# Two blocks of a head as one group, spatial products in pairs, and the last half row undivided

## The chip, the cores and the metric

The kernel runs on one core of a Trainium2 chip. The metric is device time in microseconds (us), the median of several runs; lower is better. The kernel before takes 609.88 us (three runs, 609.84 to 611.01). Engines: PE multiplies matrices (PEld is its loading of weights), DVE and ACT work on vectors, POOL is the general engine, SP issues most of the DMAs. Each engine takes its instructions strictly in the order in which they stand in its queue, so an instruction that waits holds up all behind it.

## The reference

One layer on 512 tokens of width 1024. `h = x @ w_in` is split into nine parts; branch A is a gated MLP that mixes tokens within chunks of 128, branch B is attention with two softmax maps per head.

```python
ua = gelu(ua); va = layer_norm(gelu(va), a_ln_g, a_ln_b)
sa = einsum("gts,bnsgc->bntgc", tril(w_s), va_chunks) + b_s      # 8 groups, 4 chunks
ya = ua * sa * silu(za)
q = rope(qh) * DK ** -0.5; k = rope(kh)                          # 8 heads, 2 maps, 64 wide
# for each block of 128 queries, causal:
pr = softmax(where(mask, q @ k.T, -inf)); a = pr[0] - lam * pr[1]; o = a @ v
yb = rms_norm(o, b_subln_g) * 0.8 * silu(zb)
merged = sigmoid(ga) * (ya @ w_branch_a) + sigmoid(gb) * (yb @ w_branch_b)
x = layer_norm(alpha * x + merged @ w_out + sigmoid(x @ w_ple_gate) * (p @ w_ple), ln_g, ln_b)
```

## The kernel before

All large products are made in three parts, each operand split into a high and a low piece (`three`, L279); each part is one matmul of 128 x 128 weights and 512 columns, counted by `product` (L267). These products are the stream of work on PE. Everything else is hung into the stream by hand: `later(n, fn)` (L262) puts a function on an agenda that `product` calls once n more products have been issued. What the function issues then stands at that place in every engine's queue. The numbers in the tables at the top are thus counts of products. No scheduler moves anything afterwards.

In the order of the stream: k and q of the first two heads with their rotary turn (`rope`, L694), two feature groups of ua, then v and zb (`quad`, L627: a product of halves in seven steps), then for the other three pairs of heads k, q and ua (`feature_group`, 24 products each, 144 products a pair), then za (8 x 24 products). Attention is spread over this last stretch, from the end of zb to the end of za. Then come va, ga, gb, pg, the embedding, wb, wa and the output product.

Attention works by head h and block i of 128 queries. `scores` (L763) multiplies q with k for (i + 1) x 128 keys, two maps with two matmuls each, into two `sc` banks of PSUM; DVE adds the mask and takes the row's extreme (L776, named CUSTOM_DVE_ANT_0 in the trace), ACT makes the exponentials and their sums (L782). `combine` (L786) merges the two maps on DVE (L794). `transposes` (L798) turns the result by 128 x 128 pieces into the `tr` bank and ACT copies it out as `at`. `values` (L808) multiplies it with v into the `po` bank, whose four quarters belong to the four blocks. After a head's last block, `squares` (L818), `norm`, `scale` (on POOL) and `gated` (DVE) make the normalised and gated output, and `turned` (L853) transposes it. `attention` (L871) makes a list of starts, one for each of the 32 blocks, from PERIOD (13, 16, 20, 23 products between them, 72 in all; shortened by STRETCH, 0.78, in the last two heads), and `block` (L860) hangs the steps of one block: scores at its start e, `combine` COMBINE[i] products behind, transposes at start e + 2, values at start e + 3. So at one start PE does the values of one block, the transposes of the next and the scores of the one after that; such a place, where PE leaves the stream of products and comes back, is called a point below. TAIL and LAST_TAIL (heads 5 to 7) say how far behind the last values the four steps of a head stand; `turned` stands at the start nine further.

`spatial` (L1130) makes the token mixing of branch A, one call for each of 8 groups, 17 products apart, during the product of ga: four f32 matmuls into `po` or `tr`, and 4 products later two DVE instructions that read the bank.

The output product works by rows t of 128 tokens. `fill` (L1331) has ACT put what is to be added into a bank, the first halves (512 columns) of all rows are made in two groups, then the second halves row by row. The second half of the last row is two pieces of 256 columns, each with its own bank and 24 products. Behind each piece stands `stats` (bn_stats on DVE, L1351), behind each row `last_norm` (L1353): aggregate, power on POOL, centring and scaling with the gains, and a store by SP. The last row is stored in two pieces of 512 columns.

Of the kernel before, what the change touches and what calls it, by code (L numbers as in the profile page):

```python
# [49 lines left out]
PERIOD = (13, 16, 20, 23)  # L50
COMBINE = (10, 11, 13, 12)
LAST_TURNS = (14, 27, 45)
PAIR = 144
TAIL = (2, 14, 26, 44, 56)
LAST_TAIL = (2, 10, 20, 32, 42)
# [6 lines left out]
SPATIAL = (194, 17)  # L62
# [26 lines left out]
FILL = ((14, 0, 1), (20, 2, 0), (24, 1, 1), (44, 3, 0), (110, 2, 1), (124, 3, 1), (150, 3, 2))  # L89
# [144 lines left out]
def hybrid_layer(ctx: ExitStack, tc: tile.TileContext, a, out: bass.AP):  # L234
# [528 lines left out]
    def scores(h, i):  # L763
        n = (i + 1) * P
        q, k0, k1 = stacks["q", h], stacks["k", h], stacks["kx", h]
        sc = [pbank("sc", 2) for _ in range(2)]
        for m in range(2):
            for o, kk in enumerate((k0, k1)):
                pe.matmul(sc[m][:, :n], q[:, m, i * P:(i + 1) * P], kk[:, m, :n],  # L769
                          start=o == 0, stop=o == 1)  # L770
        pr = [ap_.tile([P, T], F32, name=f"p{m}", tag=f"p{m}", bufs=3) for m in range(2)]
        if i == 0:
            todo["st", h] = small([P, NT, 4], "sth", 2)
        st = todo["st", h][:, i, :]
        for m in range(2):
            dve.tensor_tensor_reduce(out=pr[m][:, :n], in0=sc[m][:, :n], in1=mask[:, T - n:],  # L776
                                     scale=-(DK ** -0.5), scalar=3e38, op0=OP.add, op1=OP.min,
                                     accum_out=st[:, m:m + 1])
            if m == 0:
                dve.tensor_scalar(out=st[:, 0:1], in0=st[:, 0:1], scalar1=-math.log(T),  # L780
                                  scalar2=None, op0=OP.add)
            act.activation(pr[m][:, :n], pr[m][:, :n], AF.Exp, bias=st[:, m:m + 1], scale=-1.0,  # L782
                           accum_out=st[:, 2 + m:3 + m])
        todo[h, i] = pr, st

    def combine(h, i):  # L786
        n = (i + 1) * P
        pr, st = todo[h, i]
        r1 = small([P, 1], "r1")
        dve.reciprocal(out=r1, in_=st[:, 3:4])  # L790
        rho = small([P, 1], "rho")
        dve.tensor_scalar(out=rho, in0=r1, scalar1=st[:, 2:3], scalar2=neglam[:, 0:1],
                          op0=OP.mult, op1=OP.mult)
        dve.scalar_tensor_tensor(out=pr[0][:, :n], in0=pr[1][:, :n], scalar=rho[:, 0:1],  # L794
                                 in1=pr[0][:, :n], op0=OP.mult, op1=OP.add)
        todo[h, i] = pr[0]

    def transposes(h, i):  # L798
        n = (i + 1) * P
        ad = todo[h, i]  # L800
        tr = pbank("tr", 1)
        for j in range(i + 1):
            pe.transpose(tr[:, j * P:(j + 1) * P], ad[:, j * P:(j + 1) * P], ident)  # L803
        at = ap_.tile([P, T], F32, name="at", tag="at", bufs=2)
        act.activation(at[:, :n], tr[:, :n], AF.Copy)  # L805
        todo[h, i] = at

    def values(h, i):  # L808
        at = todo.pop((h, i))
        if i == 0:  # L810
            todo["po", h] = pbank("po", 1)
        po = todo["po", h]
        for j in range(i + 1):
            pe.matmul(po[:, i * P:(i + 1) * P], at[:, j * P:(j + 1) * P],  # L814
                      v[:, j, h * P:(h + 1) * P], start=j == 0, stop=j == i)

# [43 lines left out]
    def block(h, i, starts):  # L860
        e = NT * h + i
        later(starts[e], scores, h, i)
        later(starts[e] + COMBINE[i], combine, h, i)
        later(starts[e + 2], transposes, h, i)
        later(starts[e + 3], values, h, i)
        if i == NT - 1:
            tail = TAIL if h < 5 else LAST_TAIL
            for d, fn in zip(tail, (squares, norm, scale, gated)):
                later(starts[e + 3] + d, fn, h)

    def attention():  # L871
        starts = []
        for h in range(NH):
            stretch = 1.0 if h < NH - 2 else STRETCH
            at = PAIR * (h // 2) + BEGIN + h % 2 * sum(PERIOD) * stretch
            for n in PERIOD:
                starts.append(round(at))
                at += n * stretch
        starts += [starts[-1] + n for n in LAST_TURNS]
        for h in range(NH):  # L880
            for i in range(NT):
                block(h, i, starts)
# [247 lines left out]
    def spatial(g):  # L1130
# [13 lines left out]
        later(4, gated)  # L1144
# [5 lines left out]
    for g in range(KT):  # L1150
        later(SPATIAL[0] + SPATIAL[1] * g, spatial, g)
# [176 lines left out]
    last_columns = [[(0, T), (T, D)] for _ in range(NT - 1)] + [[(0, T), (T, T + T // 2), (T + T // 2, D)]]  # L1328
# [39 lines left out]
    zst = [small([P, 2 if t < NT - 1 else 3, 6], "vst", 4) for t in range(NT)]  # L1368
# [25 lines left out]
    for t in range(NT):  # L1394
# [11 lines left out]
        later(1, last_norm, t, [slice(0, D)] if t < NT - 1 else [slice(0, T), slice(T, D)])  # L1406
# [42 lines left out]
```

## Time and profile before

| what | value |
|---|---|
| median of the runs | 609.88 us |
| the profiled execution | 610.13 us |
| its span, first to last instruction | 608.2 us |
| TensorE clock granted, mean | 0.997 |
| busy share: PE, DVE, ACT, POOL | 99%, 76%, 57%, 21% |
| instructions of PE | 2880 |

Each row of a timeline gives the start and the length of an instruction in us, its engine, its line, what it writes and reads, and in brackets the idle time of the engine before it, with what ended that. A matmul's end is modelled, and the next starts before it; what a stream of matmuls costs is read from start to start. An f32 matmul (attention's values and the spatial products) stands as two instructions in the trace. A wait shows as idle time in front of the instruction that waited.

### The profile page before, as it was taken

What the parts mean: (1) busy time and instruction counts of PE and PEld (TensorE: products, weight loads), DVE (VectorE), ACT (ScalarE), POOL (GpSimd) and SP (SyncE); (2) the same over time, 40 slices, a digit from 0 to 9 for tenths busy, and PEclk for the clock granted to TensorE, in tenths of its full rate; (3) what the DMA queues carried; (4) which work ended last, traced back from release to release, by engine and by line L of the source; (5) the groups of instructions that cost most, each with busy time, mean ns of one, the idle gap of its engine ahead of it and who ended that gap; (6) DMA issues with size and microseconds to landing.
All of it is one profiled execution on the core that took longest, in us unless ns stands there. A gap on an engine that the chain in (4) does not pass through costs nothing.

```text
span 608.2 us, 8270 instructions
## 1 busy us (share of the span) xinstructions
PE 600.1 (99%) x2880; PEld 503.1 (83%) x2880; DVE 464.8 (76%) x770; ACT 346.7 (57%) x537; POOL 125.4 (21%) x133
## 2 busy tenths in 40 slices
PE   9999999999999999999999999999999999999995
PEld 6888888888888888888888888888888888888885
DVE  6995645588789789678965788779687887879476
ACT  6656475755745745746676666554776565555310
POOL 1234121041252432422110321331120011110011
PEclk9999999999999999999999999999999999999998
DMA  8689899697887896892579988976999578997002
GB/s 309 228 246 182 252 205 227 237 240 252 277 208 277 273 258 230 240 313 61 150 310 288 305 241 217 273 175 191 286 244 306 172 206 250 253 256 288 27 35 103
DMA packets 44541, 138.23 MB, mean 227 GB/s; under 512 B 5940, under 2 KB 7092, under 8 KB 44148
## 3 DMA queue, kind: packets, MB, share of 16 engines
q1 hardware_dynamic: 34436, 102.97, 46.8%
q0 software_dynamic: 9488, 34.35, 30.6%
q8 instruction: 22, 0.36, 0.2%
q10 hardware_dynamic: 576, 0.39, 0.2%
q14 instruction: 19, 0.16, 0.1%
HBM read 118.69 MB, written 29.49 MB: 244 GB/s over the span
## 4 chain that ended last, share of the span: by engine, by line
PE 98%; DVE 1%; DMA 0%; DVEq 0%; issue 0%
PE ps_pp L268 56%; PE ps_sc L268 22%; PE ps_tx L268 9%; PE ps_sc L769 3%; PE ps_po L814 3%; PE ps_tr L803 1%; PE ps_po L268 1%; PE ps_tr L268 1%; PE ps_tr L1133 1%; PE ps_po L1133 1%; PE ps_tx L857 1%; DMA xr<-in_xT 0%; PE ps_po L1319 0%; PE ps_tr L1319 0%; DVE base L1361 0%; DVE xl L295 0%
## 5 line engine op out<-in xcount | busy, mean ns | idle before, releaser
L392 DVE TENSOR_TENSOR wl<-wr,wh 128x1024 fp32r<-128x1024 f32 x133 | 165.4, 1250 | 36.7 <-ACT wh L389 36.5
L389 ACT ACTIVATE wh<-wr 128x1024 fp32r<-128x1024 f32 x133 | 139.4, 1054 | 68.7 <-PE ps_pp L268 20.5
L268 PE MATMUL ps_pp<-xh,wh 128*128 128x512 f32 x232 | 91.2, 394 | 0.0
L268 PE MATMUL ps_pp<-xh,wl 128*128 128x512 f32 x232 | 91.0, 393 | 0.0
L268 PE MATMUL ps_pp<-xl,wh 128*128 128x512 f32 x232 | 90.4, 391 | 0.1
L365 POOL DMA_DIRECT2D wr<-in_w x30 | 25.8, 872 | 153.6 <-DVE wl L392 150.6
L268 PE MATMUL ps_pp<-wl,xh 128*128 128x512 f32 (+1 forms) x148 | 56.9, 384 | 0.0
L268 PE MATMUL ps_pp<-wh,xl 128*128 128x512 f32 (+1 forms) x148 | 56.8, 384 | 0.0
L268 PE MATMUL ps_pp<-wh,xh 128*128 128x512 f32 (+1 forms) x148 | 56.7, 383 | 0.0
L782 ACT ACTIVATE p<-p,sth 128x128 f32<-128x128 f32 (+3 forms) x64 | 35.5, 556 | 28.2 <-DVE sth L780 28.0
L268 PEld LDWEIGHTS ps_pp<-xl,wh 128*128 128x128 f32 x232 | 43.6, 188 | 9.3 <-DVE xl L295 0.5
L268 PEld LDWEIGHTS ps_pp<-xh,wh 128*128 128x128 f32 x232 | 43.5, 188 | 9.0 <-ACT wh L294 0.6
L268 PEld LDWEIGHTS ps_pp<-xh,wl 128*128 128x128 f32 x232 | 43.6, 188 | 8.7
L776 DVE CUSTOM_DVE_ANT_0 p<-ps_sc,mask 128x128 f32<-128x128 f32 (+3 forms) x64 | 31.0, 484 | 19.3 <-PE ps_sc L769 19.1
L268 PE MATMUL ps_sc<-wl,xsh 128*128 128x512 f32 x88 | 34.5, 392 | 0.0
L268 PE MATMUL ps_sc<-wh,xsh 128*128 128x512 f32 x88 | 34.4, 390 | 0.0
L268 PE MATMUL ps_sc<-wh,xsl 128*128 128x512 f32 x88 | 34.3, 390 | 0.0
L805 ACT ACTIVATE at<-ps_tr 128x128 f32<-128x128 f32 (+3 forms) x32 | 13.9, 436 | 32.9 <-PE ps_tr L803 27.5
L715 POOL TENSOR_TENSOR hl<-m,hl 128x512 fp32r<-128x512 f32 x16 | 23.4, 1502 | 43.9 <-ACT hl L710 26.6
L268 PEld LDWEIGHTS ps_pp<-wl,xh 128*128 128x128 f32 x148 | 27.8, 188 | 5.4
L268 PEld LDWEIGHTS ps_pp<-wh,xh 128*128 128x128 f32 x148 | 27.8, 188 | 5.4
L268 PEld LDWEIGHTS ps_pp<-wh,xl 128*128 128x128 f32 x148 | 27.8, 188 | 5.4
(304 smaller groups left out, 1335.2 us busy)
## 6 DMA issues: line engine op xcount, KB each, us to landing
wr<-in_w SPq DMA_DIRECT2D x83, 512.0 KB, 5.2
wr<-in_w POOLq DMA_DIRECT2D x30, 512.0 KB, 6.7
wa<-in_w POOLq DMA_DIRECT2D x12, 512.0 KB, 6.2
k<-hl SPq DMA_DIRECT2D x16, 256.0 KB, 4.8
q<-hl SPq DMA_DIRECT2D x16, 256.0 KB, 3.9
ws_va<-in_w POOLq DMA_DIRECT2D x8, 512.0 KB, 9.8
wr<-ws_va SPq DMA_DIRECT2D x8, 512.0 KB, 4.7
kx<-hl SPq DMA_DIRECT2D x12, 256.0 KB, 4.5
```

The lines of the kernel that those rows point to most:

```text
L268: pe.matmul(ps, s, m, start=start, stop=stop, skip_group_check=read_within)
L365: pool.dma_start(out=raw[u], in_=weights(STEPS[FOLLOWS[u]][1]), accum_op=OP.add)
L389: act.activation(h, raw[u], AF.Copy)
L392: dve.tensor_tensor(out=l, in0=raw[u], in1=h.bitcast(F32), op=OP.subtract)
L715: pool.tensor_tensor(out=hl[:, 3 - j, :], in0=m[2 * j], in1=hl[:, j, :].bitcast(F32), op=OP.subtract)
L769: pe.matmul(sc[m][:, :n], q[:, m, i * P:(i + 1) * P], kk[:, m, :n], start=o == 0, stop=o == 1)
L776: dve.tensor_tensor_reduce(out=pr[m][:, :n], in0=sc[m][:, :n], in1=mask[:, T - n:], scale=-(DK ** -0.5), scalar=3e38, op0=OP.add, op1=OP.m ...
L782: act.activation(pr[m][:, :n], pr[m][:, :n], AF.Exp, bias=st[:, m:m + 1], scale=-1.0, accum_out=st[:, 2 + m:3 + m])
L803: pe.transpose(tr[:, j * P:(j + 1) * P], ad[:, j * P:(j + 1) * P], ident)
L805: act.activation(at[:, :n], tr[:, :n], AF.Copy)
L814: pe.matmul(po[:, i * P:(i + 1) * P], at[:, j * P:(j + 1) * P], v[:, j, h * P:(h + 1) * P], start=j == 0, stop=j == i)
L1133: pe.matmul(sa[:, t * P:(t + 1) * P], va[:, t, g * P:(g + 1) * P], aux[0][:, 0, g, :], start=True, stop=True)
```

## The change

The first two blocks of a head become one group. GROUPS lists a head's groups, each with its blocks and the columns that a block has in the two `sc` banks, the `p` tiles, the `tr` bank and `at`: blocks 0 and 1 share them (columns 0 to 127 and 128 to 383), blocks 2 and 3 stay alone. So a head has three starts instead of four, 24 in all, with PERIOD 24, 23 and 25 (72 again). The functions loop over the blocks of a group; the sums of work per head are the same. The steps of the tail are re-timed, and `turned` stands seven starts on (eight for head 6).

On PE, at the start of head 4, the kernel before has these rows (ps_po are the values, ps_tr the transposes, ps_sc the scores with k and its swapped copy kx), one point for block 0:

```order
L268 MATMUL ps_pp<-xl,wh 128x512
L814 MATMUL ps_po<-v,at 128x128 x2
L803 MATMUL ps_tr<-ident,p_1907 128x128 x3
L769 MATMUL ps_sc<-k,q 128x128
L769 MATMUL ps_sc<-kx,q 128x128
L769 MATMUL ps_sc<-k,q 128x128
L769 MATMUL ps_sc<-kx,q 128x128
L268 MATMUL ps_pp<-xh,wl 128x512
```

and 13 products on, one for block 1 (its ps_tx is the turned output of an earlier head). In the change one point stands there:

```order
L269 MATMUL ps_pp<-xl,wh 128x512
L819 MATMUL ps_po<-v,at 128x128 x3
L806 MATMUL ps_tr<-ident,p_1856 128x128 x3
L774 MATMUL ps_sc<-k,q 128x128
L774 MATMUL ps_sc<-kx,q 128x128
L774 MATMUL ps_sc<-k,q 128x128
L774 MATMUL ps_sc<-kx,q 128x128
L774 MATMUL ps_sc<-k,q 128x256
L774 MATMUL ps_sc<-kx,q 128x256
L774 MATMUL ps_sc<-k,q 128x256
L774 MATMUL ps_sc<-kx,q 128x256
L269 MATMUL ps_pp<-xh,wl 128x512
```

The scores of 256 columns have moved up to those of 128, and the values and transposes there are those of the blocks that the new starts give.

On DVE, behind the last reduction of head 7's last block, the kernel before has (wl is the low part of a weight, xt a sum of x, the RECIPROCAL and the two rows behind it are `combine`):

```order
L392 TENSOR_TENSOR wl<-wr_2698,wh 128x1024
L1016 TENSOR_TENSOR xt<-xt 128x2x256
L790 RECIPROCAL r_2957<-sth 128x1
L792 TENSOR_SCALAR rho<-r_2957,sth,neglam 128x1
L794 SCALAR_TENSOR_TENSOR p_2934<-p_2935,rho,p_2934 128x512
L851 TENSOR_TENSOR on<-on,yb 128x512
```

and the change (r0h and on are `squares`, ss and ok are `norm`, both of head 6):

```order
L825 RECIPROCAL r0h<-sth 128x4
L827 TENSOR_TENSOR on<-ps_po,r0h 128x512
L829 TENSOR_SCALAR on<-on 128x512
L393 TENSOR_TENSOR wl<-wr_2633,wh 128x1024
L1019 TENSOR_TENSOR xt<-xt 128x2x256
L839 TENSOR_REDUCE ss<-sq 128x4
L840 TENSOR_SCALAR ok<-ss 128x4
L841 TENSOR_SCALAR ss<-ss 128x4
L843 TENSOR_SCALAR ss<-ss 128x4
L793 RECIPROCAL r_2897<-sth 128x1
L795 TENSOR_SCALAR rho<-r_2897,sth,neglam 128x1
L797 SCALAR_TENSOR_TENSOR p_2855<-p_2856,rho,p_2855 128x512
```

`squares` and `norm` of head 6, which stood ahead of these reductions, have come behind them.

The spatial products come two at a time, 34 products apart, one into `po` and one into `tr`; the DVE instructions of the second stand 12 products behind, those of the first 4.

The second half of the last row is one piece of 512 columns in one bank, with one `stats`; the row is stored in pieces of 512, 256 and 256 columns. The end of DVE's queue before:

```order
L1351 BN_STATS vst<-ps_sc 128x6
L1351 BN_STATS vst<-ps_pp 128x6
L1103 BN_AGGR mv<-vst 128x2
L1104 TENSOR_SCALAR mv<-mv 128x1
L1361 SCALAR_TENSOR_TENSOR base<-ps_pp,mv,ln_g 128x512
L1361 SCALAR_TENSOR_TENSOR base<-ps_sc,mv,ln_g 128x256
L1361 SCALAR_TENSOR_TENSOR base<-ps_pp,mv,ln_g 128x256
L1365 SCALAR_TENSOR_TENSOR base<-base,rs,ln_b 128x512 x2
```

and in the change:

```order
L1354 BN_STATS vst<-ps_sc 128x6
L1106 BN_AGGR mv<-vst 128x2
L1107 TENSOR_SCALAR mv<-mv 128x1
L1364 SCALAR_TENSOR_TENSOR base<-ps_pp,mv,ln_g 128x512
L1364 SCALAR_TENSOR_TENSOR base<-ps_sc,mv,ln_g 128x512
L1368 SCALAR_TENSOR_TENSOR base<-base,rs,ln_b 128x512
L1368 SCALAR_TENSOR_TENSOR base<-base,rs,ln_b 128x256 x2
```

One statistics instruction and one centring are gone, and the last shift stands as two.

The diff, cut to its core:

```diff
-PERIOD = (13, 16, 20, 23)
-COMBINE = (10, 11, 13, 12)
+GROUPS = (((0, slice(0, 128)), (1, slice(128, 384))), ((2, slice(0, 384)),), ((3, slice(0, 512)),))
+PERIOD = (24, 23, 25)
+COMBINE = (15, 13, 12)
-TAIL = (2, 14, 26, 44, 56)
-LAST_TAIL = (2, 10, 20, 32, 42)
+TAIL = (2, 14, 24, 37)
+LATE_TAIL = (2, 10, 19, 30, 42)
-SPATIAL = (194, 17)
+SPATIAL = (194, 34)
-FILL = ((14, 0, 1), (20, 2, 0), (24, 1, 1), (44, 3, 0), (110, 2, 1), (124, 3, 1), (150, 3, 2))
+FILL = ((14, 0, 1), (20, 2, 0), (24, 1, 1), (44, 3, 0), (110, 2, 1), (124, 3, 1))
...
+    def scores(h, g):
...
+        for i, cs in GROUPS[g]:
+            for m in range(2):
+                for o, kk in enumerate((k0, k1)):
+                    pe.matmul(sc[m][:, cs], q[:, m, i * P:(i + 1) * P], kk[:, m, :cs.stop - cs.start],
+                              start=o == 0, stop=o == 1)
+        for i, cs in GROUPS[g]:
+            st = todo["st", h][:, i, :]
+            for m in range(2):
+                dve.tensor_tensor_reduce(out=pr[m][:, cs], in0=sc[m][:, cs], in1=mask[:, T - (cs.stop - cs.start):],
...
+                act.activation(pr[m][:, cs], pr[m][:, cs], AF.Exp, bias=st[:, m:m + 1], scale=-1.0,
+                               accum_out=st[:, 2 + m:3 + m])
...
+    def group(h, g, starts):
+        e = len(GROUPS) * h + g
+        later(starts[e], scores, h, g)
+        later(starts[e] + COMBINE[g], combine, h, g)
+        later(starts[e + 2], transposes, h, g)
+        later(starts[e + 3], values, h, g)
+        if g == len(GROUPS) - 1:
+            for d, fn in zip(TAIL if h < 4 else LATE_TAIL, (squares, norm, scale, gated)):
                 later(starts[e + 3] + d, fn, h)
...
-            later(starts[NT * h + 9], turned, h)
-        later(starts[-1] + LAST_TAIL[4], turned, NH - 1)
+            later(starts[3 * h + (7 if h < NH - 2 else 8)], turned, h)
+        later(starts[-1] + LATE_TAIL[4], turned, NH - 1)
...
-        later(4, gated)
+        later(4 + 8 * (g % 2), gated)
...
-        later(SPATIAL[0] + SPATIAL[1] * g, spatial, g)
+        later(SPATIAL[0] + SPATIAL[1] * (g // 2), spatial, g)
...
-    last_columns = [[(0, T), (T, D)] for _ in range(NT - 1)] + [[(0, T), (T, T + T // 2), (T + T // 2, D)]]
+    last_columns = [[(0, T), (T, D)] for _ in range(NT - 1)] + [[(0, T), (T, D)]]
...
-        later(1, last_norm, t, [slice(0, D)] if t < NT - 1 else [slice(0, T), slice(T, D)])
+        later(1, last_norm, t, [slice(0, D)] if t < NT - 1 else [slice(0, T), slice(T, T + T // 2), slice(T + T // 2, D)])
```

More of the change, by code (lines that the diff above doesn't have):

```diff
@@ L761, in hybrid_layer @@
     todo = {}
-    def scores(h, i):
-        n = (i + 1) * P
+    def scores(h, g):
         q, k0, k1 = stacks["q", h], stacks["k", h], stacks["kx", h]
         sc = [pbank("sc", 2) for _ in range(2)]
[L767 to L770, printed above, removed]
         pr = [ap_.tile([P, T], F32, name=f"p{m}", tag=f"p{m}", bufs=3) for m in range(2)]
-        if i == 0:
+        if g == 0:
@@ L773, in scores @@
             todo["st", h] = small([P, NT, 4], "sth", 2)
[L774 to L796, printed above, removed]
@@ L798, in transposes @@
-    def transposes(h, i):
-        n = (i + 1) * P
-        ad = todo[h, i]
+        todo[h, g] = pr
+        for i, cs in GROUPS[g]:
[7 more added lines that the diff above has]
+                dve.tensor_tensor_reduce(out=pr[m][:, cs], in0=sc[m][:, cs], in1=mask[:, T - (cs.stop - cs.start):],
+                                         scale=-(DK ** -0.5), scalar=3e38, op0=OP.add, op1=OP.min,
+                                         accum_out=st[:, m:m + 1])
+                if m == 0:
+                    dve.tensor_scalar(out=st[:, 0:1], in0=st[:, 0:1], scalar1=-math.log(T),
+                                      scalar2=None, op0=OP.add)
+                act.activation(pr[m][:, cs], pr[m][:, cs], AF.Exp, bias=st[:, m:m + 1], scale=-1.0,
+                               accum_out=st[:, 2 + m:3 + m])
@@ new lines, in combine @@
+    def combine(h, g):
+        pr = todo[h, g]
+        for i, cs in GROUPS[g]:
+            st = todo["st", h][:, i, :]
+            r1 = small([P, 1], "r1")
+            dve.reciprocal(out=r1, in_=st[:, 3:4])
+            rho = small([P, 1], "rho")
+            dve.tensor_scalar(out=rho, in0=r1, scalar1=st[:, 2:3], scalar2=neglam[:, 0:1],
+                              op0=OP.mult, op1=OP.mult)
+            dve.scalar_tensor_tensor(out=pr[0][:, cs], in0=pr[1][:, cs], scalar=rho[:, 0:1],
+                                     in1=pr[0][:, cs], op0=OP.mult, op1=OP.add)
+        todo[h, g] = pr[0]
@@ L801, in transposes @@
+    def transposes(h, g):
+        ad = todo[h, g]
         tr = pbank("tr", 1)
-        for j in range(i + 1):
-            pe.transpose(tr[:, j * P:(j + 1) * P], ad[:, j * P:(j + 1) * P], ident)
+        n = GROUPS[g][-1][1].stop
+        for c in range(0, n, P):
+            pe.transpose(tr[:, c:c + P], ad[:, c:c + P], ident)
         at = ap_.tile([P, T], F32, name="at", tag="at", bufs=2)
         act.activation(at[:, :n], tr[:, :n], AF.Copy)
[L806 to L810, printed above, removed]
+        todo[h, g] = at
@@ L811, in values @@
+    def values(h, g):
+        at = todo.pop((h, g))
+        if g == 0:
             todo["po", h] = pbank("po", 1)
         po = todo["po", h]
-        for j in range(i + 1):
-            pe.matmul(po[:, i * P:(i + 1) * P], at[:, j * P:(j + 1) * P],
-                      v[:, j, h * P:(h + 1) * P], start=j == 0, stop=j == i)
+        for i, cs in GROUPS[g]:
+            for j in range(i + 1):
+                c = cs.start + j * P
+                pe.matmul(po[:, i * P:(i + 1) * P], at[:, c:c + P], v[:, j, h * P:(h + 1) * P],
+                          start=j == 0, stop=j == i)
@@ L858, in turned @@
         act.activation(yb[:, h, :], tr, AF.Copy, scale=g08[:, 0:1])
[L860 to L868, printed above, removed]
+    def group(h, g, starts):
[6 more added lines that the diff above has]
+            for d, fn in zip(TAIL if h < 4 else LATE_TAIL, (squares, norm, scale, gated)):
                 later(starts[e + 3] + d, fn, h)
@@ L880, in attention @@
         for h in range(NH):
-            for i in range(NT):
-                block(h, i, starts)
+            for g in range(len(GROUPS)):
+                group(h, g, starts)
         for h in range(NH - 1):
-            later(starts[NT * h + 9], turned, h)
-        later(starts[-1] + LAST_TAIL[4], turned, NH - 1)
+            later(starts[3 * h + (7 if h < NH - 2 else 8)], turned, h)
+        later(starts[-1] + LATE_TAIL[4], turned, NH - 1)
     later(LAMBDAS[0], load_constants)
@@ L1366, in last_norm @@
             sp.dma_start(out=out[t * P:(t + 1) * P, cs], in_=z)
-    zst = [small([P, 2 if t < NT - 1 else 3, 6], "vst", 4) for t in range(NT)]
+    zst = [small([P, 2, 6], "vst", 4) for t in range(NT)]
     units = []
```

## The prediction

> **What bounds the kernel now.** I read the page's busy times and its chain first, then the waits of PE, then the timeline at the places that the change touches.
>
> ```profile
> span 608.2 us, 8270 instructions
> PE 600.1 (99%) x2880; PEld 503.1 (83%) x2880; DVE 464.8 (76%) x770; ACT 346.7 (57%) x537; POOL 125.4 (21%) x133
> PE 98%; DVE 1%; DMA 0%; DVEq 0%; issue 0%
> PE ps_po L462 <- DVE zeros L459: 1.3, 1, 1.3
> ```
>
> PE works for 600.1 of 608.2 us, 98% of the chain that ended last is PE, and the only wait of PE that the trace has is 1.3 us before its first instruction. So nothing can make this kernel much faster but fewer or shorter PE steps, or a shorter tail behind the last matmul; and all that DVE, ACT, POOL and the queues do stays free until a result that PE needs comes late. The profiled execution took 610.13 us, its span and 1.93 us around it; it lies 0.25 us above the median of the runs shown, 609.88. I make the sum against 610.13 and take the 0.25 off at the end.
>
> **Fewer points at which PE leaves its stream of products.** The scores, transposes and values of a head, and the spatial products, stand between products of 512 columns. The change takes no such matmul away: blocks 0 and 1 of a head keep their eight score matmuls (128 and 256 columns), three transposes and three value matmuls, now at one point instead of two. What goes is the cost of a point itself, at 8 points of attention (24 instead of 32) and 4 of the spatial products (4 pairs instead of 8). The PE timeline around a spatial point, with start and length in front:
>
> ```profile
> 388.51 0.39 PE L268 MATMUL ps_pp<-wl,xh 128*128 128x512 f32 x1
> 388.74 1.05 PE L1133 MATMUL ps_po<-aux,va 128*128 128x128 f32 x8
> 389.55 0.48 PE L268 MATMUL ps_pp<-wh,xl 128*128 128x512 f32 x1
> 389.86 0.40 PE L268 MATMUL ps_pp<-wh,xh 128*128 128x512 f32 x1
> 390.10 0.39 PE L268 MATMUL ps_pp<-wl,xh 128*128 128x512 f32 x1
> ```
>
> A product starts 0.23 us after the one before it (388.51 to 388.74). From 388.51 to 390.10 stand three such steps and the point: 1.59 - 3 x 0.227 = 0.91 us for 8 instructions. Eight bare steps are to be taken from that; their length shows in the attention point of block 0 of a head:
>
> ```profile
> 226.79 0.39 PE L268 MATMUL ps_pp<-xl,wh 128*128 128x512 f32 x1
> 227.02 0.60 PE L814 MATMUL ps_po<-v,at 128*128 128x128 f32 x4
> 227.46 0.49 PE L803 MATMUL ps_tr<-ident,p 128*128 128x128 f32 x3
> 227.71 0.31 PE L769 MATMUL ps_sc<-k,q 128*128 128x128 f32 x1
> ...
> 228.19 0.45 PE L268 MATMUL ps_pp<-xh,wl 128*128 128x512 f32 x1
> ...
> 228.71 0.39 PE L268 MATMUL ps_pp<-xl,wh 128*128 128x512 f32 x1
> ```
>
> Four value instructions take 0.44 us (227.02 to 227.46), 0.111 each. The spatial point is then 8 x 0.111 = 0.89, and 0.02 us is left for leaving the stream and coming back. Here, from 226.79 to 228.71 are 1.92 us; less three products of 0.227 this leaves 1.24 us for 4 + 3 + 4 instructions, and 11 x 0.111 = 1.22: again 0.02. So 12 points less give 12 x 0.02 = 0.24 us. The bounds: nothing at the one end; at the other the 0.087 by which the first product behind a point (389.55 to 389.86, 0.31) is longer than 0.227, 12 x 0.087 = 1.04. I take 0.24, because the sums over whole points give it: the longer first step is made up by the last f32 instruction, which the next product follows at once.
>
> **The last half row in one group.** Its 48 products of 256 columns become 24 of 512. The end of the kernel, PE, DVE, POOL and the queue of SP:
>
> ```profile
> 595.31 0.39 PE L268 MATMUL ps_sc<-wh,xl 128*128 128x512 f32 x1
> 595.53 0.28 PE L268 MATMUL ps_sc<-wh,xh 128*128 128x256 f32 x1
> ...
> 601.16 0.28 PE L268 MATMUL ps_pp<-wh,xl 128*128 128x256 f32 x1
> 601.48 0.43 DVE L1351 BATCH_NORM_STATS2 vst<-ps_pp 128x6 f32<-128x256 f32 x1 [0.57 <-PE ps_pp L268]
> 601.95 0.24 DVE L1103 BATCH_NORM_AGGREGATE mv<-vst 128x2 f32<-128x18 f32 x1
> 602.29 0.74 DVE L1361 SCALAR_TENSOR_TENSOR base<-ps_pp,mv,ln_g 128x512 f32<-128x512 f32 x1
> 602.45 0.54 POOL L1106 TENSOR_TENSOR rs<-mv,mhalf 128x1 f32<-128x1 f32 x1 [3.20 <-DVE mv L1104]
> 602.95 0.47 DVE L1361 SCALAR_TENSOR_TENSOR base<-ps_sc,mv,ln_g 128x256 f32<-128x256 f32 x1
> 603.73 1.41 DVE L1365 SCALAR_TENSOR_TENSOR base<-base,rs,ln_b 128x512 f32<-128x512 f32 x2
> 604.50 0.99 SPq L1366 DMA_DIRECT2D out<-base  x2
> ```
>
> Before, the last product starts (601.16 - 595.53) = 5.63 us after the first, 47 steps of 0.120, and ends 0.28 later: 5.91. After, 23 steps of 0.227 and 0.39 (the row at 595.31): 5.61. PE ends 0.30 us earlier. [...]
>
> **The tail behind it.** The statistics of 512 columns stand in the row before, with the aggregate of two pieces:
>
> ```profile
> 596.53 0.69 DVE L1351 BATCH_NORM_STATS2 vst<-base 128x6 f32<-128x512 f32 x1
> 597.26 0.21 DVE L1103 BATCH_NORM_AGGREGATE mv<-vst 128x2 f32<-128x12 f32 x1
> 597.58 1.27 DVE L1361 SCALAR_TENSOR_TENSOR base<-base,mv,ln_g 128x1024 f32<-128x1024 f32 x1
> ...
> out<-base SPq DMA_DIRECT2D x2, 512.0 KB, 2.6
> out<-base SPq DMA_DIRECT2D x2, 256.0 KB, 2.0
> ```
>
> Statistics: 0.73 from start to start (596.53 to 597.26) instead of 0.47 (601.48 to 601.95): +0.26. Aggregate and EPS: 0.32 instead of 0.34: -0.02. Centring from the banks: two of 512 at 0.66 each (602.29 to 602.95) instead of 512 + 256 + 256 in 1.44 (602.29 to 603.73): -0.12. The scale by `rs` doesn't wait: POOL had it at 602.99. Shift: 512 + 256 + 256, some 0.12 longer than 512 + 512 by the same difference with its sign turned: +0.12. So the last store is issued 0.24 later behind PE's end, 0.06 earlier in all. That store is half as large. The nearest rows, 2.6 us for 512 KB and 2.0 for 256 KB, fall by 0.3 per 128 KB if that line goes on (1.7), and by nothing if 2.0 is the floor; I take the middle, -0.15, and keep both ends. SP takes a third issue: two take 0.99 us with a wait for DVE between them, so one is under 0.5, and the shifts are 0.4 apart; the last issue comes late by 0 to 0.2, and I take 0.1. The removed ACT fill and the second statistics (in front of PE's end) were hidden and give nothing.
>
> Sum: -0.24 - 0.30 + 0.24 - 0.15 + 0.10 = -0.35 us; 610.13 - 0.35 = 609.8, less 0.25 is **609.5 us**.
>
> **Why no new wait of PE is counted.** By the tables, the products between a block's `combine` and its `transposes` were 19, 25, 30 and 24; now they are 32, 35 and 37 (STRETCH shortens both in heads 6 and 7). `squares` has 23 products to read the bank before `values` of the next head writes it, 18 before. `gated` and `turned` are 12 products apart, as before, in heads 0 to 3. Group 0 puts four reductions in a row on DVE and four exponentials on ACT; the next scores, which need the two banks back, come 24 products later, 5.4 us, and the rope products queued behind them on DVE read banks that PE writes again a whole feature group later. SP's DMAs stand in the same order, but for the last stores. On POOL the powers of `norm` in heads 1 and 3 move behind the two subtractions of a rope (the row below, 1.5 each), those of heads 4 and 5 behind one issue of an accumulating DMA; the subtractions are due 9 products, 2.0 us, ahead of `norm`, so about 1 us of their 3.0 is left when it is issued, its reduce runs beside that, and `turned` needs the outcome only 35 products, 7.9 us, behind `norm`. In pairs, the spatial banks `po` and `tr` come back within 12 products of the 34 before the next pair. The place with the least room is the last block of head 7, where `squares` and `norm` of head 6 now stand between its reductions and its `combine`:
>
> ```profile
> 280.05 0.18 DVE L821 RECIPROCAL r0h<-sth 128x4 f32<-128x4 f32 x1
> 281.33 0.69 DVE L1016 TENSOR_TENSOR xt<-xt 128x512 f32<-128x512 f32 x1
> 282.17 0.69 DVE L835 TENSOR_REDUCE ss<-sq 128x4 f32<-128x512 f32 x1 [0.16 <-ACT sq L827]
> 284.42 0.68 DVE L776 CUSTOM_DVE_ANT_0 p<-ps_sc,mask 128x512 f32<-128x512 f32 x1
> 285.82 2.35 DVE L392 TENSOR_TENSOR wl<-wr,wh 128x1024 fp32r<-128x1024 f32 x1
> ...
> 285.76 1.32 POOL L847 TENSOR_TENSOR on<-on,f 128x512 f32<-128x512 f32 x1
> ...
> 282.85 0.47 PE L769 MATMUL ps_sc<-k,q 128*128 128x512 f32 x1
> 291.46 0.60 PE L803 MATMUL ps_tr<-ident,p 128*128 128x128 f32 x4
> L392 DVE TENSOR_TENSOR wl<-wr,wh 128x1024 fp32r<-128x1024 f32 x133 | 165.4, 1250 | 36.7 <-ACT wh L389 36.5
> L715 POOL TENSOR_TENSOR hl<-m,hl 128x512 fp32r<-128x512 f32 x16 | 23.4, 1502 | 43.9 <-ACT hl L710 26.6
> ```
>
> PE goes from these scores to these transposes in 8.6 us, the same 27 products and one point afterwards. DVE then has: first bank ready some 0.75 after the scores start (estimate: two matmuls), reductions 1.4 (284.42 to 285.82), `squares` 1.3 (280.05 to 281.33), `wl` 1.25, `xt` 0.69, and reduce with the small ones and a combine 2.3 (282.17 to 284.42), 0.1 more for 512 columns: 7.8 us. So 0.8 us of room are left. The bank of head 6's values has a little more: `values` of head 7 write it 12 products after `squares`, some 4.1 us after these scores start (4 x 0.23 + 14 x 0.227), and DVE has read it after 0.75 + 1.4 + 0.9 = 3.05.
>
> **Rivals.** *A point costs its long first step (faster).* Then 12 x 0.087 = 1.04 instead of 0.24, and with a store that lands at 1.7 the sum is -1.04 - 0.30 + 0.24 - 0.30 + 0.10 = -1.3: 608.6 us. For it: each first product behind a point does show 0.3. Against it: the sums over whole points, and that starts alone are measured on PE. I give it 0.12.
>
> *POOL holds DVE in that last block (slower).* The row at 285.82 has `wl` at 2.35 us, 1.1 above its mean, beside POOL's scaling at 285.76; both read two tensors from SBUF. If `scale` and `pow` of the head meet DVE there, and `wl`, `xt` and the combine's last step each lose 1.1, DVE is 3.3 late, over the 0.8 of room by 2.5, and PE waits that long: 609.5 + 2.5 = 612.0 us. It decides from 0.8 us on, and makes the kernel slower than before from 1.2. Against it: `scale` needs the reduce, which now stands behind `wl`, so it comes after two of the three. I give it 0.07. [...]
>
> *The tail gives the gain back.* The store lands no sooner than 2.0 (+0.15), and POOL's `rs` comes late by the few tenths that separate 0.54 from a longer power: 610.0 us, still no change. I give it 0.11.
>
> **How the numbers follow.** A measurement of this kernel can tell about 0.2%, 1.2 us, from no change: 608.7 to 611.1. My forecast, no new wait and small terms, has 0.70 and lies within; with the third rival 0.81 for the same. Faster needs the first rival, 0.12; slower the second, 0.07. The forecast's own terms reach from 609.1 (store at 1.7 and a little more per point) to 609.9 (no gain at the points, store at 2.0). For 8 in 10 I go to 608.5 below, which takes in the first rival, and to 610.6 above, a wait of 1 us at the last block.
>
> **What would show it.** Right: PE's list of waits still has only the first 1.3 us; 2856 PE records; points of head groups of about 2.0 us for 6 + 3 + 8 instructions; the last product starts 5.2 us after the first of its half row; the span is 0.3 to 0.7 shorter. Wrong: a new row of PE waits, on DVE's `p` or `on` (then the second rival, at 290 us), or a gap before the first shift; a span shorter by over 1.2 us would say that a point costs more than whole points sum to.

## The result

The kernel became slower, by a little: 611.92 us median of 22 runs (610.65 to 613.03) against 610.41 us of the kernel before beside it (22 runs, 609.84 to 611.89). The ratio is 1.0022, its 95% interval 1.0015 to 1.0029; so it is 0.9 to 1.8 us slower, where 609.5 us was forecast, 0.35 us faster by the sum. The profiled execution took 612.13 us, its span is 610.4 (608.2 before), its granted clock 0.996.

### The profile page after: what moved, and what is told of

The parts are those of the page before. It is cut to its first block, busy times and chain, and to the rows that moved or that the text cites. A ratio compares the mean times of both kernels' runs of the same rounds, so it can differ in the third digit from the quotient of the medians.

```text
span 610.4 us, 8202 instructions
## 1 busy us (share of the span) xinstructions
PE 600.4 (98%) x2856; PEld 501.5 (82%) x2856; DVE 461.1 (76%) x769; ACT 343.9 (56%) x528; POOL 119.3 (20%) x133
## 4 chain that ended last, share of the span: by engine, by line
PE 89%; DMA 4%; DVE 3%; issue 1%; ACT 1%; POOL 0%; SPq 0%; ACTq 0%; DVEq 0%; POOLq 0%
PE ps_pp L269 50%; PE ps_sc L269 21%; PE ps_tx L269 8%; PE ps_sc L774 3%; PE ps_po L819 2%; DMA pt<-in_pT 2%; DMA q<-hl 1%; PE ps_tr L806 1%; PE ps_po L269 1%; PE ps_tr L269 1%; DMA wr<-in_w 1%; DVE wl L393 1%; PE ps_tr L1136 1%; PE ps_po L1136 1%; DVE p L779 0%
## 5 line engine op out<-in xcount | busy, mean ns | idle before, releaser
L269 PE MATMUL ps_pp<-wh,xl 128*128 128x512 f32 x140 | 54.6, 390 | 0.0
L269 PE MATMUL ps_pp<-wh,xh 128*128 128x512 f32 x140 | 54.5, 389 | 0.0
L269 PE MATMUL ps_pp<-wl,xh 128*128 128x512 f32 x140 | 54.5, 389 | 0.0
L808 ACT ACTIVATE at<-ps_tr 128x384 f32<-128x384 f32 (+1 forms) x24 | 12.7, 528 | 40.1 <-PE ps_tr L806 37.5
L269 PEld LDWEIGHTS ps_pp<-wh,xh 128*128 128x128 f32 x140 | 26.3, 188 | 5.5
L269 PEld LDWEIGHTS ps_pp<-wh,xl 128*128 128x128 f32 x140 | 26.3, 188 | 5.4
L269 PEld LDWEIGHTS ps_pp<-wl,xh 128*128 128x128 f32 x140 | 26.3, 188 | 5.4
```

Source lines behind the costliest of these rows:

```text
L269: pe.matmul(ps, s, m, start=start, stop=stop, skip_group_check=read_within)
```

## The profile after

The head of the page and the chain of the changed kernel, then its whole list of PE's waits (us in total, times, longest):

```profile
span 610.4 us, 8202 instructions
PE 600.4 (98%) x2856; PEld 501.5 (82%) x2856; DVE 461.1 (76%) x769; ACT 343.9 (56%) x528; POOL 119.3 (20%) x133
...
PE 89%; DMA 4%; DVE 3%; issue 1%; ACT 1%; POOL 0%; SPq 0%; ACTq 0%; DVEq 0%; POOLq 0%
```

```profile
PE ps_po L463 <- DVE zeros L460: 1.3, 1, 1.3
PE ps_sc L774 <- DMA q<-hl: 1.0, 1, 1.0
PE ps_pp L269 <- ACT wh L295: 0.5, 1, 0.5
PE ps_sc L269 <- ACT s L637: 0.2, 1, 0.2
```

There are 2856 PE records, as forecast, but DMA now holds 4% of the chain (0 before), and three rows have joined the list of waits. The one for `wh` (0.5) stands at 6.4 us, ahead of all that was changed; the one for q (1.0) at 251 us; the one for `s` (0.2) at 449 us, where PE loses 0.51 us from start to start. By place, comparing starts with starts in the two traces: 0.81 us are lost before the first scores (117.05 before, 117.86 now), where nothing was changed; heads 0 to 5 are 0.26 shorter; head 6 loses 1.13; head 7 up to the last turn 0.20; from there to the last half row 0.36; the end 0.03. That makes 2.27, and the spans differ by 2.26.

The 0.36 are more than one thing: 0.51 are lost at 449, and 0.27 are won around 470 us, where 48 products of the embedding (`phl`) take 10.88 us instead of 11.15. No term of the sum has these 0.27. They are there in each of the eight kernels of this document with the last half row undivided, and in none of the five with the divided one, run 4's among these; why, no run here shows.

**The wait for q.** SP writes the turned `q` into its place with four stores around 245 us (the stacks, L732); the first scores of head 6 read what the second of them brings. PE, changed kernel:

```profile
251.13 0.28 PE L774 MATMUL ps_sc<-kx,q 128*128 128x128 f32 x1
252.37 0.30 PE L774 MATMUL ps_sc<-k,q 128*128 128x128 f32 x1 [0.96 <-DMA q<-hl]
```

POOL, then the first pair of SP's stack stores and the middle time of all four from issue to landing (last column) at that place, before:

```profile
244.51 1.95 POOL L840 TENSOR_TENSOR f<-ss,mhalf 128x4 f32<-128x4 f32 x1 [0.51 <-DVE ss L839]
247.80 1.75 POOL L324 DMA_DIRECT2D ws_pg<-in_w  x2
244.02 1.18 SPq L731 DMA_DIRECT2D q<-hl  x2
...
q<-hl SPq DMA_DIRECT2D x4, 256.0 KB, 3.3
```

and in the changed kernel:

```profile
243.64 0.85 POOL L325 DMA_DIRECT2D ws_pg<-in_w  x1
250.19 1.03 POOL L844 TENSOR_TENSOR f<-ss,mhalf 128x4 f32<-128x4 f32 x1 [5.70 <-DVE r L793]
243.72 1.18 SPq L732 DMA_DIRECT2D q<-hl  x2
...
q<-hl SPq DMA_DIRECT2D x4, 256.0 KB, 7.3
```

Before, POOL's queue held the accumulating DMA of `ws_pg` (one that adds what it brings to what lies there) back behind the power `f` and the scaling of head 4, which waited for DVE; it went out at 247.80, with the stacks already moving. In the change it stands ahead of that power, goes out at 243.64, beside the first stacks, and these land after 7.3 us instead of 3.3. The second stack lands 7.9 us after its issue instead of 2.4, at 252.24, and PE goes on at 252.37.

**The wait at 449 us.** ACT cuts pT, the transposed input of the embedding, and in the change waits for its load; SP's two loads of pT before, the same now, and ACT now:

```profile
pt<-in_pT SPq DMA_DIRECT2D x2, 256.0 KB, 6.8
```

```profile
pt<-in_pT SPq DMA_DIRECT2D x2, 256.0 KB, 11.6
447.39 0.63 ACT L295 ACTIVATE phl<-pt 128x512 fp32r<-128x512 f32 x1 [1.83 <-DMA pt<-in_pT]
```

**The end**, with DVE's last instructions and the three stores (half and full pieces to landing):

```profile
602.98 0.39 PE L269 MATMUL ps_sc<-wh,xl 128*128 128x512 f32 x1
603.41 0.70 DVE L1354 BATCH_NORM_STATS2 vst<-ps_sc 128x6 f32<-128x512 f32 x1 [0.60 <-PE ps_sc L269]
604.14 0.21 DVE L1106 BATCH_NORM_AGGREGATE mv<-vst 128x2 f32<-128x12 f32 x1
604.45 0.74 DVE L1364 SCALAR_TENSOR_TENSOR base<-ps_pp,mv,ln_g 128x512 f32<-128x512 f32 x1
605.11 0.74 DVE L1364 SCALAR_TENSOR_TENSOR base<-ps_sc,mv,ln_g 128x512 f32<-128x512 f32 x1
605.77 1.53 DVE L1368 SCALAR_TENSOR_TENSOR base<-base,rs,ln_b 128x512 f32<-128x512 f32 x3
...
out<-base SPq DMA_DIRECT2D x1, 256.0 KB, 2.0
out<-base SPq DMA_DIRECT2D x2, 128.0 KB, 2.1
```

The last product starts 5.21 us after the first of its half row (forecast 5.2), and the span ends 7.44 us behind it (7.00 before). From the first product of the half row to the end are 12.66 us, 12.63 before. A store of 128 KB (2.1 us) takes as long as one of 256 KB (2.0).

## The experiments

The theory at the start: the accumulating DMA and the stacks collide, and that is the largest part. Beside it stood a theory for the second wait, at 449 us (the spatial pairs make loads late), and chance as its rival.

**1. The DMA back behind the power, in the changed kernel.**

```diff
-'pg': (320, 430)
+'pg': (320, 432)
```

> The changed kernel, with one number moved: the first accumulating DMA of the summed weights pg is due at 432 instead of 430, so that on POOL it stands behind the power of head 4's norm again, as before the change. Theory of the collision: this DMA, issued at 243.6 us, shares the DMA engines with the four stores of the turned q stacks (issued 243.7 to 248.4), which therefore land after 7.3 us instead of 3.3, and PE waits 1.13 us for them at the scores of head 6. Then here the stacks land in 3 to 4 us, the wait at 251 us is gone, and the time is 1.1 to 1.4 us under the changed kernel (ratio to before about 1.0002 to 1.0005). Rival, the stacks are late because SP's queue is late (it waits longer ahead of the loads of wr): the landing stays at 6 to 7 us, PE still waits about 1 us, time as the changed kernel (1.0022).

Measured: ratio to before 1.0008 (1.0000 to 1.0017), 610.94 us. Beside PE's first wait its list has only this one:

```profile
PE ps_tx L269 <- ACT ps_tx L649: 0.5, 1, 0.5
```

The stacks land in 3.3 us and the wait for them is gone, though SP issues them as far apart as in the changed kernel (243.09 and 246.53 us; 243.72 and 247.18 there). The kernel was still not as fast as the one before, as far as the interval tells: the wait shown stands at 524 us, where ACT's cut of a weight had waited 3.76 us for its load, and 0.19 us are lost at 461.

**2. The same DMA forward, in the kernel before.**

```diff
-'pg': (320, 430)
+'pg': (320, 416)
```

> The kernel before, with one number moved the other way: that DMA is due at 416 instead of 430, so that it stands ahead of the power of head 4's norm, as in the changed kernel; nothing else of the change is in. Theory of the collision: the q stacks land after 6 to 8 us, PE waits 0.5 to 1.5 us at the scores of head 6, about 250.5 us, and the kernel is about 1 us slower than before (ratio 1.0010 to 1.0025). Rival (SP's queue, or the order of the blocks, makes the stacks late): landing 3 to 4 us, no wait, ratio 1.000.

Measured: ratio 1.0074 (1.0061 to 1.0086), 614.93 us: the collision is there without the rest of the change, and costs 4.5 us where about 1 was expected. Waits and landing, and then PE behind the wait:

```profile
PE ps_sc L769 <- DMA q<-hl: 2.5, 1, 2.5
```

```profile
q<-hl SPq DMA_DIRECT2D x4, 256.0 KB, 11.2
```

```profile
253.59 0.30 PE L769 MATMUL ps_sc<-k,q 128*128 128x128 f32 x1 [2.53 <-DMA q<-hl]
...
253.83 0.65 PE L268 MATMUL ps_pp<-xh,wl 128*128 128x512 f32 x1
254.28 0.63 PE L268 MATMUL ps_pp<-xh,wh 128*128 128x512 f32 x1
```

The wait is 2.7 us beyond the bare steps (start to start), and eight products behind it take 0.43 us each instead of 0.227, 1.6 us more: 4.3 of the 4.5 us that the ratio makes.

**3. The spatial products one by one, in the changed kernel.**

```diff
-SPATIAL = (194, 34)
+SPATIAL = (194, 17)
...
-        later(4 + 8 * (g % 2), gated)
+        later(4, gated)
...
-        later(SPATIAL[0] + SPATIAL[1] * (g // 2), spatial, g)
+        later(SPATIAL[0] + SPATIAL[1] * g, spatial, g)
```

> The changed kernel with the spatial products one by one again, 17 products apart, as before the change; the rest of the change is in. Theory that the pairs make the load of pT late (11.6 us instead of 6.8 from issue to landing, beside two accumulating loads of POOL that came 3 us later than before, so that PE waits 0.5 us at 449 us): here the load lands in 6 to 8 us, the wait at 449 is gone, the time is 0.4 us under the changed kernel (ratio to before 1.0015). Rival, the lateness of that load is chance or comes from the attention part: it shows up here too, or shows up in some of these four kernels without regard to the edit; time as the changed kernel but for four points (0.02 to 0.1 us each, slower).

Measured: ratio 1.0011 (1.0002 to 1.0020), 610.94 us. pT lands after 6.9 us, nothing is lost at 449, and beside PE's first wait only the one for q is left in the list:

```profile
PE ps_sc L774 <- DMA q<-hl: 0.9, 1, 0.9
```

**4. The last row as before, in the changed kernel.**

```diff
-    last_columns = [[(0, T), (T, D)] for _ in range(NT - 1)] + [[(0, T), (T, D)]]
+    last_columns = [[(0, T), (T, D)] for _ in range(NT - 1)] + [[(0, T), (T, T + T // 2), (T + T // 2, D)]]
...
-slice(0, T), slice(T, T + T // 2), slice(T + T // 2, D)]
+slice(0, T), slice(T, D)]
```

(with the third fill and the third statistics that belong to it)

> The changed kernel with the last half row in two groups of 256 columns and stored in two pieces, as before the change; the rest of the change is in. From the traces, the time from the first product of the half row to the end was 12.57 us before and 12.60 after: so here the same time as the changed kernel within 0.1 us, with 6.9 us from the last product's start to the end instead of 7.4. Rival, the new tail costs: 0.3 us or more under the changed kernel. The start of the kernel is the same in all four kernels: if the first scores, 117.05 us before and 117.86 after, scatter between these values here too, the 0.8 us there are chance and not the change's.

Measured: ratio 1.0033 (1.0021 to 1.0046), 612.37 us from 5 runs, 0.45 over the changed kernel where 0.1 was expected; the intervals overlap. From the first product of the half row to the end are 12.64 us, so the tail costs and brings nothing, as expected. What differs lies elsewhere: two late waits, at 437 and 463 us, which cost 1.29 us together, where the changed kernel's profile has 0.51 at 449, and the 0.27 us at the embedding's products, which are not won here. The first scores of these four kernels start at 117.21, 117.25, 117.23 and 117.13 us: the changed kernel's 117.86 is not the change's. The kernels of later runs, with and without the change, lie between 117.03 and 117.98.

**5. Both edits: the DMA behind the power, spatial products one by one** (the diffs of 1 and 3).

> The changed kernel with both edits that took a wait away: the accumulating DMA behind the power of head 4's norm (due 432), and the spatial products one by one, 17 apart. What is left of the change is the attention groups and the last half row. If these two are all that made the change slow, PE has no wait but the first 1.3 us and some 0.2 us at the last turn, its last product starts at 600.4 to 600.8 us (601.63 with the spatial products alone undone, less 1.03 of the wait for q), and the time is that of before or a little under: ratio 0.999 to 1.0002. Rival, a further cost is left in the attention groups or the last row: ratio 1.0008 or more, and a wait or a longer tail that shows it.

Measured: ratio 0.9994 (0.9985 to 1.0002), 610.13 us; no wait of PE in its list but the first 1.3 us. Its last product starts later than expected, 601.30 instead of 600.4 to 600.8, because its first scores start at 117.98. So the two edits account for the loss; the interval is too wide to say more of what is left.

**6. The spatial pairs alone, in the kernel before** (the diff of 3 with its signs turned).

> The kernel before with the spatial products in pairs and nothing else of the change. Theory: the four additions and products of a pair stand on DVE within 8 products, the low parts of the weights behind them come late, so POOL's accumulating loads are issued 4 to 9 products (1 to 2 us) later (in the changed kernel: behind product 1602 of the feature products instead of 1593, 1643 instead of 1639, 1658 instead of 1652), and some load between 425 and 530 us lands too late, at a place that differs from run to run: PE waits 0.3 to 1.1 us in all there, less four points of 0.02 to 0.09, ratio 1.0002 to 1.0018. Rival, the pairs only hurt together with the attention groups, or those waits were chance: no wait of PE in 425 to 530 us, ratio 0.9993 to 1.0000.

Measured: ratio 1.0010 (1.0001 to 1.0019), 611.37 us, and the runs spread from 610.05 to 612.21 (the kernel before beside it from 609.77 to 612.11, but with a median of 610.34). The profiled execution took 610.34 us, near the lower end, with only 0.27 us lost at 460 us, so what the slower executions waited for is not shown. What it shows is the lateness that the theory starts from. DVE and POOL before:

```profile
422.56 0.68 DVE L641 TENSOR_TENSOR s<-s,ps_tx 128x512 f32<-128x512 f32 x1
423.16 1.22 DVE L392 TENSOR_TENSOR wl<-wr,wh 128x1024 fp32r<-128x1024 f32 x1
424.30 0.69 DVE L1139 TENSOR_TENSOR y<-ps_tr,aux 128x512 f32<-128x512 f32 x1
425.02 0.69 DVE L1142 TENSOR_TENSOR ua<-ua,y 128x512 f32<-128x512 f32 x1
...
424.68 0.87 POOL L365 DMA_DIRECT2D wr<-in_w  x1 [12.48 <-DVE wl L392]
427.15 0.85 POOL L365 DMA_DIRECT2D wr<-in_w  x1 [1.59 <-DMA gate_gb<-s]
...
438.06 0.85 POOL L365 DMA_DIRECT2D wr<-in_w  x1 [2.13 <-DVE wl L392]
```

and with the pairs:

```profile
423.27 0.68 DVE L1139 TENSOR_TENSOR y<-ps_tr,aux 128x512 f32<-128x512 f32 x1
423.99 0.69 DVE L1142 TENSOR_TENSOR ua<-ua,y 128x512 f32<-128x512 f32 x1
424.60 0.68 DVE L641 TENSOR_TENSOR s<-s,ps_tx 128x512 f32<-128x512 f32 x1
425.19 2.35 DVE L392 TENSOR_TENSOR wl<-wr,wh 128x1024 fp32r<-128x1024 f32 x2
...
426.71 0.88 POOL L365 DMA_DIRECT2D wr<-in_w  x1 [15.13 <-DVE wl L392]
427.85 0.85 POOL L365 DMA_DIRECT2D wr<-in_w  x1 [0.26 <-DMA gate_gb<-s]
...
439.16 0.85 POOL L365 DMA_DIRECT2D wr<-in_w  x1 [2.27 <-DVE wl L392]
```

The last spatial product's two DVE instructions (y, ua), 12 products behind the pair instead of 17 + 4, have moved ahead of `s` and of `wl`. The `wl` that releases POOL's accumulating load starts at 425.19 instead of 423.16, that load goes out 2.0 us later, and the following ones 0.7 to 1.1.

**7. Pairs, with the second read by DVE where it was read before** (on the kernel of run 1).

```diff
-        later(4 + 8 * (g % 2), gated)
+        later(4 + 17 * (g % 2), gated)
```

> The changed kernel with the accumulating DMA due at 432, and the spatial products still in pairs, but the second of each pair read by DVE 21 products behind it instead of 12, that is at the product at which it was read before the change. If it is DVE's four operations close together that delay the loads, POOL's accumulating loads are back at their products (1593, 1639, 1652 within 2), PE does not wait in 425 to 530 us, and with the four points saved it is as fast as the kernel with single spatial products or 0.1 to 0.3 us faster: ratio 0.9985 to 1.0000. Rival, it is the pair on PE itself, or chance: waits of 0.3 to 1.1 us there, ratio about 1.0008 as with the accumulating DMA moved alone.

Measured: ratio 0.9994 (0.9985 to 1.0002), 610.14 us. DVE's order is back, and with it the time: the kernel of run 1, which differs only by this number, was at 1.0008. POOL's three loads come 0.75, 0.53 and 0.74 us later than before, though (425.43, 435.60 and 438.80 us, the first scores at 117.03 and 117.05; behind products 1597, 1642 and 1656, 3 or 4 later than before, so the bound of 2 is missed), and 0.44 us are lost at 461 us, no less than in the one profile of run 6. So by the times DVE's order is the larger part; where the rest of the lateness comes from, no run here shows.

**8. The last row in two pieces, on the kernel of run 7.**

```diff
-[slice(0, T), slice(T, T + T // 2), slice(T + T // 2, D)]
+[slice(0, T), slice(T, D)]
```

> The kernel of the run with the gates apart, with the last row stored in two pieces of 512 columns instead of 512 and two of 256. A store of 128 KB landed in 2.1 us and one of 256 KB in 2.0, so the third piece should save nothing: the last store is issued some 0.1 us earlier here, and the end lies 0.1 us earlier behind the last product (7.3 instead of 7.4 us); the time is the same within what can be measured. Rival, the half-size store is worth the 0.15 us that was forecast: the end comes 0.1 us or more later than with three pieces.

Measured: ratio 0.9993 (0.9985 to 1.0002), 610.17 us. The end stands 7.22 us behind the last product's start instead of 7.44, and 12.44 behind the first product of the half row: the third piece costs 0.22 us, twice what was expected.

**9. POOL's two DMAs for pg as plain copies, in the changed kernel.**

```diff
-pool.dma_start(out=there[n, j], in_=source, accum_op=OP.add, max_dma_last_dim=4096)
+pool.dma_start(out=there[n, j], in_=source, max_dma_last_dim=4096, **({} if name == 'pg' else dict(accum_op=OP.add)))
```

> The changed kernel with the two DMAs of POOL that add to the summed weights pg made plain copies of the same size, at the same places of the same queue (so pg's weights are not the sums, and the gate pg is computed from others). If it is the amount that they move beside the stores of the turned q, the stacks still land after about 7 us and PE waits about 1 us at 251 us: ratio to before about 1.002. If it is the adding that slows the other queue, the stacks land in 3 to 5 us, the wait is 0 to 0.3 us, and the ratio is about 1.0008, as with the DMA moved behind the power.

Measured: ratio 1.0003 (0.9994 to 1.0013), 611.03 us; PE does not wait for q (0.4, 0.3 and 0.7 us are lost at 436, 446 and 462 us, where the other kernels with pairs lose theirs).

```profile
ws_pg<-in_w POOLq DMA_DIRECT2D x2, 512.0 KB, 4.8
q<-hl SPq DMA_DIRECT2D x4, 256.0 KB, 4.6
```

A copy of the same size at the same place delays the stacks by 1.3 us, the adding one by 4.0 (the second stack, which PE waits for, by 2.4 and 5.5): it is the adding.

**10. Only the first of the two DMAs forward, in the kernel before** (due at 416; the second at 442, as before).

> The kernel before with only the first of the two accumulating DMAs of pg ahead of the power of head 4's norm; the second stands where it stood before the change. In the run where both came sooner PE stood 2.5 us for the stacks, and then eight products took 0.427 us each instead of 0.227 at a granted clock near 0.5, 1.6 us more. If each of the two adds its part and the clock falls only behind a long stand, here the stacks land in 5 to 8 us, PE waits 0 to 1.5 us, no product behind it takes 0.4 us, and the ratio to before is 1.000 to 1.0025. Rival, the first one alone does it all: landing 11 us, wait 2.5 us, slow products, ratio 1.007.

Measured: ratio 1.0041 (1.0025 to 1.0057), 613.04 us, between the two, with the landing near the rival's.

```profile
PE ps_sc L769 <- DMA q<-hl: 1.9, 1, 1.9
```

```profile
q<-hl SPq DMA_DIRECT2D x4, 256.0 KB, 10.6
```

The first one does nearly all of the lateness (10.6 of 11.2 us; 8.0 of 8.6 for the second stack, the one that PE waits for); so the second adds little to it. The products behind the wait, 2.0 us from start to start, take 0.227 us again in this profile, so the slow ones of run 2 go with its longer stand.

**11. All three costs undone** (the diffs of 1, 3 and 8).

> The changed kernel with all three of its costs undone: the accumulating DMA due at 432, the spatial products one by one, the last row stored in two pieces. From the kernel with two pieces, the time from the first product of the last half row to the end is 12.44 us instead of 12.65 before; the attention groups save eight points, 0.3 to 0.6 us; the last turn's wait of 0.2 us stays. Expected: no wait of PE but the first 1.3 us, 0.3 to 0.7 us under the kernel before, ratio 0.9988 to 0.9996. Rival, the gain lies within what can be told from no change: ratio 0.9997 or more.

Measured: ratio 0.9984 (0.9975 to 0.9993), 609.51 us (609.25 to 610.11): faster than both kernels, by somewhat more than expected, with a span of 607.6 us. Its list has one row beside PE's first wait, 0.2 us at 5.1 us, ahead of all that was changed. What came with the groups of attention and the undivided half row had eaten the gain.

Where the gain lies is not as expected, though. Its trace is 0.59 us shorter than that of the kernel before: 0.31 are won in attention up to head 7's first scores, but 0.23 of them are lost again at the last turn; 0.27 are won at the embedding's 48 products, and 0.18 from the first product of the last half row to the end. The medians differ by more, 1.1 us: the profiled execution of the kernel before was one of its quick ones. Its span is 608.2 us, and the 15 executions beside this run have spans from 608.2 to 609.5, with a median of 608.8.

## Why the prediction was wrong

The failed step is **"Why no new wait of PE is counted"**, at two sentences.

- "those of heads 4 and 5 [move] behind one issue of an accumulating DMA" and "SP's DMAs stand in the same order". Both are true, and both were read only for what they do to the power and to SP's queue. When a power moves behind a DMA, the DMA moves ahead of the power, and ahead of the power's wait for DVE: it left POOL at 243.64 us instead of 247.80, into the stacks' transfer. PE then waited 1.13 us at 251 us, which the prediction put at nothing. Undoing that alone took the wait away (run 1), doing it alone brought it into the kernel before (runs 2 and 10).
- "In pairs, the spatial banks `po` and `tr` come back within 12 products". The banks did. What was not followed is the place of those DVE instructions among the others: ahead of a `wl` that releases a load of POOL (run 6). PE then waits for a load, at places that differ from run to run: between 425 and 530 us each of the five profiles with the pairs and gates 12 products behind them loses 0.3 to 1.5 us (449 us in the changed kernel, 461 and 524 in run 1, 437 and 463 in run 4, 460 in run 6, 436, 446 and 462 in run 9), and none of the six with single products loses any (before, runs 2, 3, 5, 10 and 11). With the gates apart one of two does (0.5 in run 7, none in run 8).

The two cost, by the ratios, about 0.0014 (run 1 against the changed kernel, 0.9 us) and 0.0011 (run 3 against it, 0.7 us), each to within some 0.001. Both undone are at 0.9994, where the sum without waits, -0.35 of 610, also lies (0.9994). That they meet is luck. By the traces of run 5 and the kernel before, 0.24 us lost at the last turn and 0.27 won at the embedding's products, neither of them in the sum, nearly cancel, and the tail, which gives back 0.14 more than forecast, is made up by the eight points of attention, which bring 0.31 instead of 0.16.

The terms of the sum itself:

- *PE bounds the kernel*: held (busy for 600.4 of 610.4 us), and so each of PE's waits showed in the time.
- *A point costs 0.02 us*: too small for attention. From the first scores of head 3 to those of head 6 the kernel before takes 68.18 us (182.26 to 250.44), the changed one 68.02 (182.97 to 250.99): 0.053 for each of three points, between the two ends given (0.26 over the first six heads, 0.04 each). The first rival, 0.087 at each point, was no nearer. At the spatial products, four points fewer brought 0.00 to 0.05 us in all (the changed kernel and runs 1, 6 and 7, from 380 to 430 us).
- *The last half row ends 0.30 us earlier on PE*: right. From the first product's start to the last's are 5.21 us instead of 5.63, and the last is 0.11 longer.
- *The tail, +0.24 to the last shift*: right in its parts (statistics 0.73, aggregate with EPS 0.31, centring 0.66 each).
- *Half the store, -0.15, and the third issue, +0.10*: wrong in sign. 128 KB landed in 2.1 us where 256 KB took 2.0, so halving the store brought nothing here; three pieces instead of two cost 0.22 (run 8). The third rival, that the tail gives its gain back, came true in the time, 12.66 us instead of 12.63, but only half in its reasons: the store landed no sooner, POOL's `rs` was there before the shift, and the rest is the third piece.
- *The last block of head 7*, the second rival: no wait of PE stands at 290 us. DVE's later order shows only at the last turn, where PE goes from a product to the turn in 0.44 us (307.63 to 308.07) instead of 0.23: DVE's `squares` of head 7 read the values 2.8 us after PE starts them instead of 1.1, and the steps up to the turn hang on that.

A wait on DVE's `p` or `on`, named as the sign of error, was the wrong sign to watch; the rows that the change brought were a DMA and ACT behind a DMA.

## What to carry to other kernels

When an order changes on a queue that issues DMAs, follow each DMA both ways: what is later because of it, and what it now goes out ahead of, since a wait in front of it may have been what kept it out of another transfer's way (here a DMA of POOL that left 4.2 us sooner, and a stack that landed after 7.9 us instead of 2.4). Follow side work (here DVE's gates) to the loads that it releases, not only to the banks it reads; here, with the DMA engines 0.97 and 0.98 busy from 425 to 450 and from 450 to 475 us of the changed kernel, 1 to 2 us of lateness there came back as waits at places that changed from run to run. Compare a profile's span with those of the other executions, since it can be that of a quick one (here 608.2 us, where 15 others had a median of 608.8). Before halving a store at the end, look whether the smaller of two sizes already lands no sooner (here 128 KB in 2.1 us, 256 KB in 2.0).

## What the runs showed of the hardware

**The accumulating DMA kept the engines busy and moved less.** From 246 to 248 us (columns from the right: GB/s, busy share of the DMA engines, granted clock), before and after:

```profile
246.00:248.00 2.00, 2.00 (x11) 1.65 (x10) 0.98 (x6) 1.57 (x5) 1.84 (x4) 1.00 0.92 286
```

```profile
246.00:248.00 2.00, 2.00 (x10) 1.69 (x9) 1.93 (x4) 0.58 (x2) 0.00 (x0) 1.00 0.87 131
```

The engines are about as busy (0.87 against 0.92) and move less than half (131 against 286 GB/s). The packets in the traces show what fills them. An adding packet of 4 KB takes 0.33 us (the middle one of the 128), a copying one of the same size in run 9 0.16, one of a stack, 2 KB, 0.08. And from 245.9 to 248.9 us of the changed kernel no packet of SP's queue that carries data starts, while 109 adding ones do; runs 2, 3 and 10 have the same gap, 3.0 to 3.2 us long. Both kinds do start from 255 to 260 us of the kernel before, 194 adding packets and 208 of 2 KB of SP's. Why adding packets hold an engine longer, and why SP's queue stands at first, no run here shows.

**Behind a stand of 2.7 us the clock was halved.** The windows of run 2, with the granted clock in the third column from the right:

```profile
250.00:253.40 3.40, 1.06 (x10) 0.91 (x8) 0.45 (x3) 3.36 (x6) 0.00 (x0) 1.00 1.07 295
253.40:257.00 3.60, 3.41 (x10) 2.77 (x11) 2.73 (x7) 0.78 (x4) 0.00 (x0) 0.57 1.05 244
257.00:261.00 4.00, 4.00 (x28) 3.59 (x27) 0.93 (x5) 1.63 (x6) 0.00 (x0) 0.96 0.78 258
```

The clock was 0.57 over the 3.6 us behind the stand; by the trace's record of it, it was half for 3.41 us from 253.91. All five executions of run 2 have a mean clock of 0.994 or 0.995, the kernel before beside them 0.996 to 0.999. In the profiles with stands of 1.0 to 2.0 us (the changed kernel, runs 3, 4 and 10) it stayed at full speed, but two of the six executions of run 10, whose profile has the 2.0, have a mean of 0.995, the others 0.997 or 0.998. In run 2 the halving followed a stand of 2.7 us, 2.53 of them idle; what the shortest stand is that does it, no run here shows.
